# One sweep for the first layer's q, k and v, the norm chain moved ahead, and joined halves only from the memory's keys on

## The chip, the core and the metric

The kernel runs on one core of a Trainium2 chip. The metric is the device time of one execution in microseconds. TensorE (PE) multiplies, VectorE (DVE) and ScalarE (ACT) feed it and clear its results, POOL (GpSimd) does powers and some transfers, SP issues most loads.

## The reference

The program is a two-layer attention block followed by a hybrid mixer, a cross attention and an MLP, on 256 tokens of width 1024 in float32. The change touches the first layer, of which this is the core:

```python
h = rmsnorm(x, norm_gain[l])
mk, mv = jnp.split(memn @ w_mem_kv[l], 2, axis=-1)
...
qa, ka, va, qb, kb, vb, qm, gate = split_cols(h @ w_in_even[e], SPLIT_EVEN)
qa = rope_2d(rmsnorm(qa.reshape(B, S, A_HEADS, HEAD_DIM), q_norm_a[e]), grid_row, grid_col)
ka = rope_2d(rmsnorm(ka.reshape(B, S, A_KV, HEAD_DIM), k_norm_a[e]), grid_row, grid_col)
ya = global_gqa(qa, ka, va.reshape(B, S, A_KV, HEAD_DIM))
yb = window_gqa(...)
ym = memory_attn(qm.reshape(B, S, M_HEADS, M_HEAD_DIM), mk, mv)
y = jnp.concatenate([ya, yb, ym], axis=-1) * jax.nn.silu(gate)
x = x + y @ w_out_even[e]
```

## The kernel before

Each float32 operand is split in two: a high part rounded to the type that PE takes at full speed, and a low part, the difference. A product is then three matmuls: high x high, high x low, low x high (`mm3`). ACT writes the high part of a weight (`t_wh<-t_raw`), DVE the low part (`t_wl<-t_raw,t_wh`); both come from a weight tile `t_raw` that SP loads. There are three buffers for `t_raw` and four each for `t_wh` and `t_wl`; twenty-four slots of 4 KB hold the other operands.

Where the activations are the moving operand (`proj_t`), `merge` decides the form. With `merge` on, `proj_sum` lays the high and low part of the activations beside each other, so that one matmul of 512 columns does two of the three products and one of 256 columns the third; the two halves of the PSUM bank are then added by an ACT copy and a DVE add into `t_sum`. With `merge` off there are three matmuls of 256 columns into one place, and the readers take PSUM itself.

The first layer begins without the norm. The tokens come transposed (`t_xT`), two row blocks of 128 at a time, each followed by the weights of k, v and the window's v (384 columns, `t_mm` in two banks). `turn` multiplies by the norm's gain and splits (`t_gh<-t_xT,t_gT`). All eight row blocks are swept for these 384 columns, and later swept again for q (512 columns). The norm itself is applied to the results: squares of the tokens on ACT (`t_sq`), a sum and a reduce on DVE (`t_y<-t_sq`), a matmul with ones that sums over partitions (`t_at<-t_ones,t_y`), a power on POOL (`t_rstd`), and a matmul that spreads the result over partitions (`t_at<-t_p,t_ones`). From that DVE and ACT make the normed tokens `t_xs` and their halves `t_hT`, which the window's k (`kb`), the gate (`gate_tile`), and the memory's query (`mem_q`) use. `window_bias` makes a table with a one-hot matmul and stores it to DRAM. The rotations (`rope`) of k and q and the memory's norm are put between the projections in small steps.

The order of the instructions isn't the order in the text. `Plan` records all operations, then `order` puts them in a list with a cost model: each engine takes the ready operation of lowest priority number, which is the place in the text plus a `bias` and a `SHIFT` for a kind of tile. The list is issued as it stands, and each engine runs its part in order. Loads share one modelled queue with 450 ns each. Before the first data arrive, PE runs `WARM` matmuls on zeros.

Of the kernel before, what the change touches and what calls it, by code (L numbers as in the profile page):

```python
# [10 lines left out]
F32 = mybir.dt.float32  # L11
# [5 lines left out]
P = 128  # L17
# [12 lines left out]
class Plan:  # L30
# [13 lines left out]
    def __init__(self, nc):  # L44
        import concourse.bacc as bacc
        self.nc = nc
        self.names = bacc.Bacc("TRN2", target_bir_lowering=False, num_devices=1)
        self.ops, self.tiles, self.last, self.bias, self.ahead = [], {}, None, 0, False
        for e in self.ENGINES:
            setattr(self, e, Plan.Engine(self, e))  # L50
# [80 lines left out]
    def cost(self, engine, method, args, kwargs, outs, ins):  # L131
# [14 lines left out]
        if engine == "scalar":  # L146
            return n / 1.2 + (93 if sbuf else 51) + 94 * col + 93 * accum, 0.0, 0
# [14 lines left out]
    def order(self, prio):  # L162
# [12 lines left out]
        avail = {e: (2000.0 if e == "scalar" else 600.0, -1) for e in self.ENGINES}  # L175
        ring, bus = 0.0, 0.0
# [23 lines left out]
        while len(seq) < n:  # L200
# [19 lines left out]
            if o["bytes"]:  # L220
                if e != "gpsimd":
                    ring = max(ring, t) + 450.0
                    avail[e] = (ring, i)
                    bus = max(bus, ring + 650.0)
# [83 lines left out]
class Kernel:  # L308

    def __init__(self, ctx, tc, a, out):  # L310
        self.tc, self.nc, self.a, self.out = tc, Plan(tc.nc), a, out

        class Pool:

            def __init__(pool, name, bufs, space=None):
                pool.space = space
                pool.real = ctx.enter_context(tc.tile_pool(name=name, bufs=bufs, **({"space": space} if space else {})))

            def tile(pool, shape, dtype, tag=None, name=None, bufs=1):
# [12 lines left out]
        self.rate = 0.0  # L332
        self.merge = True
# [34 lines left out]
    def consts(self):  # L368
# [15 lines left out]
        early = self.work("st", [P, 8], 8)  # L384
        nc.scalar.activation(early, self.mhalf, AF.Exp)
        self.ident = self.c[:, C_ID:C_ID + P]

# [23 lines left out]
    def window_bias(self):  # L411
# [7 lines left out]
        oh = self.work("tanh", [33, 512], 2)  # L419
        nc.sync.dma_start(oh, a["onehot"])  # L420
        u = self.psum("at")
        uf = u.rearrange("p a b -> p (a b)")
        nc.tensor.matmul(uf[:8, :], rb, oh, start=True, stop=True)
        us = self.work("tanh", [8, 512], 2)
        nc.scalar.activation(us, uf[:8, :], AF.Copy, scale=-1.0)
        self.wb = self.dr.tile([8, 512], F32, name="wb")
        nc.sync.dma_start(self.wb, us)
# [108 lines left out]
    def spread(self, r, b):  # L536
# [274 lines left out]
    def gate_tile(self, w, c0, hT):  # L811
# [3 lines left out]
        for i in range(2):  # L815
            po = self.proj_t(w, c0 + i * 256, hT)
# [181 lines left out]
    def layer_even(self):  # L998
# [5 lines left out]
        def pieces():  # L1004
            for k0 in range(0, KT, 2):
                nc.ahead = True
                nc.sync.dma_start(self.xT[k0 // 4][:, k0 % 4:k0 % 4 + 2, :],
                                  a["x_t"][k0 * P:(k0 + 2) * P].rearrange("(k p) s -> p k s", p=P))
                nc.ahead = False
                raw = self.wp.tile([P, 2, 384], F32, tag="raw", name=self.name("raw"), bufs=3)  # L1010
                rs = slice(k0 * P, (k0 + 2) * P)
                for d, c0, n in ((0, 512, 256), (256, 1408, 128)):
                    nc.sync.dma_start(raw[:, :, d:d + n], w_in[rs, c0:c0 + n].rearrange("(k p) c -> p k c", p=P))
                turn(k0)
                turn(k0 + 1)
                yield k0, raw
                if k0 == TAB:
                    self.tab = self.rope_tables()

        po = self.proj_n(pieces(), KT, 384, xg)  # L1020
# [14 lines left out]
        self.window_bias()  # L1035
# [11 lines left out]
        pq = self.proj_n(self.wide(w_in, 0, KT, 0, step=2), KT, 512, xg)  # L1047
# [4 lines left out]
        kb = self.k_stack(self.proj_t(w_in, 1280, hT, P), 1)  # L1052
# [10 lines left out]
        g["a"] = self.gate_tile(w_in, 2048, hT)  # L1063
# [6 lines left out]
        self.flush("mem")  # L1070
        mk = self.mem_k(w_kv[0], self.mem1)
# [328 lines left out]
WARM = 20  # L1400
SHIFT = {("tensor", "mm"): 100, ("vector", "wl"): -20}
TAB = 4
BIAS = [40, 80, 110, 0, 0]
# [87 lines left out]
```

## Time and profile before

| | us |
|---|---|
| three runs | 779.42, 780.11, 781.4 (median 780.11) |
| the profiled execution | 779.68 |
| its span in the trace | 777.9 |
| PE busy | 763.1 (98%) |
| DVE busy | 620.0 (80%) |
| ACT busy | 536.8 (69%) |
| POOL busy | 74.7 (10%) |

The profiled execution's own time is 1.8 us above its span, for what lies around the instructions that the trace records. Nearly every operation is issued by one line of the program (L284), so rows are told apart by their tiles: `t_wl<-t_raw,t_wh` is the instruction that writes the low half of a weight. In a timeline row stand the start, the busy time, the engine, the operation, the shape, how many were merged into the row, and in brackets the idle time before it with what ended it. A matmul's busy time overlaps with the next, so its price is read from one start to the next.

### The profile page before, as it was taken

The numbers are of one execution on the slowest core, as the hardware profiler recorded it, in microseconds if no ns is written. First come the engines' busy times: TensorE is split into PE (matmuls) and PEld (weight loads), VectorE is DVE, ScalarE is ACT, GpSimd is POOL, SyncE is SP. The second block draws the span as 40 slices with busy tenths as digits, with TensorE's granted clock in tenths as the row PEclk, the third lists the DMA queues.
The fourth block names the chain that finished last, engine by engine and source line by source line (L and its number), as shares of the span: only waits on it lengthen the run. The fifth ranks groups of instructions, "written<-read, shape, count | busy, mean of one in ns | idle before, by whom it ended". The sixth has DMA issues, their size and how long they took to land.

```text
span 777.9 us, 11758 instructions
## 1 busy us (share of the span) xinstructions
PE 763.1 (98%) x4320; PEld 661.2 (85%) x4320; DVE 620.0 (80%) x1127; ACT 536.8 (69%) x1046; POOL 74.7 (10%) x105
## 2 busy tenths in 40 slices
PE   8989999999999999999999999999999999999996
PEld 7678898888888888888888898799989888888885
DVE  5999998998779889979988889976677655565554
ACT  6697987876679669757787787465556765556552
POOL 0640010000001421132011100100000000000000
PEclk9999999999999999999999999999999999999998
DMA  7796546445558855765348645356535565655631
GB/s 231 244 285 216 162 127 227 138 137 176 184 186 260 237 159 157 210 202 190 115 156 242 191 120 193 105 179 217 181 118 164 177 185 180 215 191 187 210 115 54
DMA packets 109989, 140.48 MB, mean 181 GB/s; under 512 B 3779, under 2 KB 81539, under 8 KB 109932
## 3 DMA queue, kind: packets, MB, share of 16 engines
q1 hardware_dynamic: 104460, 131.64, 52.5%
q0 software_dynamic: 5472, 8.10, 4.7%
q8 instruction: 34, 0.56, 0.3%
q14 instruction: 23, 0.19, 0.1%
HBM read 134.98 MB, written 1.06 MB: 175 GB/s over the span
## 4 chain that ended last, share of the span: by engine, by line
PE 86%; DVE 5%; issue 3%; POOL 2%; ACT 2%; DMA 1%; SPq 0%; POOLq 0%; DVEq 0%; ACTq 0%
PE t_mm L284 64%; PE t_at L284 22%; DVE t_wl L284 2%; DVE t_y L284 1%; POOL t_rrs L284 1%; POOL t_rstd L284 1%; DMA t_xT<-in_x_t_dram 1%; POOL t_ks L284 1%; ACT t_wh L284 0%; DVE t_xs L284 0%; DVE t_p L284 0%; DVE t_x L284 0%; ACT t_p L284 0%; ACT t_xg L284 0%; ACT t_mT L284 0%
## 5 line engine op out<-in xcount | busy, mean ns | idle before, releaser
L284 DVE TENSOR_TENSOR t_wl<-t_raw,t_wh 128x1024 fp32r<-128x1024 f32 (+1 forms) x237 | 288.8, 1219 | 72.6 <-ACT t_wh L284 70.9
L284 ACT ACTIVATE t_wh<-t_raw 128x1024 fp32r<-128x1024 f32 (+1 forms) x237 | 250.4, 1058 | 74.2 <-PE t_mm L284 61.3
L284 PE MATMUL t_mm<-t_mT,t_wh 128*128 128x512 f32 (+1 forms) x512 | 181.6, 394 | 0.4 <-ACT t_wh L284 0.4
L284 PE MATMUL t_mm<-t_mT,t_wl 128*128 128x256 f32 x496 | 131.9, 284 | 0.0
L284 PE MATMUL t_mm<-t_wh,t_yh 128*128 128x512 f32 x288 | 113.5, 394 | 0.0
L284 PE MATMUL t_mm<-t_wh,t_yl 128*128 128x512 f32 x288 | 112.9, 393 | 0.0
L284 PE MATMUL t_mm<-t_wl,t_yh 128*128 128x512 f32 x288 | 112.7, 391 | 0.0
L284 PEld LDWEIGHTS t_mm<-t_mT,t_wh 128*128 128x128 f32 x512 | 93.7, 188 | 14.0 <-ACT t_wh L284 0.8
L284 PEld LDWEIGHTS t_mm<-t_mT,t_wl 128*128 128x128 f32 x496 | 93.4, 189 | 6.5 <-DVE t_wl L284 0.3
L284 PE MATMUL t_at<-t_mT,t_wh 128*128 128x512 f32 (+1 forms) x256 | 85.7, 382 | 0.0
L284 ACT COPY t_sum<-t_mm 128x256 f32<-128x256 f32 x97 | 36.0, 371 | 55.6 <-PE t_mm L284 55.1
L284 PE MATMUL t_mm<-t_wh,t_gh 128*128 128x256 f32 (+2 forms) x256 | 65.9, 339 | 1.5 <-ACT t_wh L284 1.5
L284 PE MATMUL t_at<-t_mT,t_wl 128*128 128x256 f32 x240 | 63.8, 280 | 0.0
L284 PEld LDWEIGHTS t_mm<-t_wh,t_yl 128*128 128x128 f32 x288 | 54.1, 188 | 11.1
L284 PEld LDWEIGHTS t_mm<-t_wl,t_yh 128*128 128x128 f32 x288 | 54.1, 188 | 10.8
L284 PEld LDWEIGHTS t_mm<-t_wh,t_yh 128*128 128x128 f32 x288 | 54.1, 188 | 10.5 <-ACT t_yh L284 0.2
L284 PE MATMUL t_mm<-t_hT,t_wh 128*128 128x512 f32 x168 | 61.8, 400 | 1.0 <-DVE t_sum L284 1.0
L284 ACT ACTIVATE t_p<-t_p,t_st 128x256 f32<-128x256 f32 (+1 forms) x111 | 52.6, 493 | 9.6 <-DVE t_st L284 9.4
L284 POOL TENSOR_TENSOR t_rstd<-t_rstd,t_mhalf 128x2 f32<-128x2 f32 (+1 forms) x12 | 13.3, 1107 | 457.3 <-DVE t_rstd L284 457.3
L284 PEld LDWEIGHTS t_at<-t_mT,t_wh 128*128 128x128 f32 x256 | 45.8, 188 | 6.8
L284 DVE TENSOR_TENSOR t_sum<-t_mm,t_sum 128x256 f32<-128x256 f32 x97 | 40.8, 421 | 13.5 <-ACT t_sum L284 12.7
L284 PEld LDWEIGHTS t_mm<-t_wh,t_gh 128*128 128x128 f32 x256 | 45.1, 194 | 5.9 <-ACT t_wh L284 1.7
(177 smaller groups left out, 1389.1 us busy)
## 6 DMA issues: line engine op xcount, KB each, us to landing
t_raw<-in_w_in_odd_dram SPq DMA_DIRECT2D x20, 1024.0 KB, 5.2
t_raw<-in_w_up_dram SPq DMA_DIRECT2D x16, 1024.0 KB, 5.7
t_raw<-in_w_down_dram SPq DMA_DIRECT2D x16, 1024.0 KB, 5.0
t_raw<-in_w_in_dram SPq DMA_DIRECT2D x12, 1024.0 KB, 5.5
t_raw<-in_w_in_even_dram SPq DMA_DIRECT2D x10, 1024.0 KB, 5.1
t_raw<-in_w_mem_kv_dram SPq DMA_DIRECT2D x8, 1024.0 KB, 5.2
t_raw<-in_w_out_even_dram SPq DMA_DIRECT2D x6, 1024.0 KB, 5.6
t_raw<-in_w_out_odd_dram SPq DMA_DIRECT2D x6, 1024.0 KB, 5.3
```

The lines of the kernel that those rows point to most:

```text
L284: f(*[self.real(v) for v in args], **{k: self.real(v) for k, v in kwargs.items()})
```

## The change

The columns of both sweeps are taken in one pass: for each row block the 512 columns of q and the 384 of k and v, in four banks at once. The first two row blocks come one at a time, the first weight in two pieces; the gains and the first two blocks of tokens are loaded from ACT's queue, the rest of the tokens from SP's. The plan gives each engine its own load queue, starts ACT at 600 ns like the others, and charges the table load to the first activation. The norm chain has a bias of -200. `merge` starts off and is turned on before the first memory's keys. The projections of `kb` and of the gate write the banks named `at`. The one-hot matmul moves behind the gate. The diagonal of the spread may go to ACT or DVE. There are 24 warm-up matmuls instead of 20.

```diff
-        avail = {e: (2000.0 if e == "scalar" else 600.0, -1) for e in self.ENGINES}
-        ring, bus = 0.0, 0.0
+        avail = {e: (600.0, -1) for e in self.ENGINES}
+        ring, bus = {e: 0.0 for e in self.ENGINES}, 0.0
...
-        self.merge = True
+        self.merge = False
...
-        nc.sync.dma_start(self.g, a["gains"])
+        nc.scalar.dma_start(self.g, a["gains"])
         self.xT = [self.slot([P, 4, S], "xT", F32) for _ in range(2)]
+        for k in range(2):
+            self.load_x(k, 1, nc.scalar)
...
-            nc.vector.tensor_scalar(diag[:, t, :], self.ident, r[:, t:t + 1], None, ALU.mult)
+            self.scaled(diag[:, t, :], self.ident, r[:, t:t + 1])
...
-        po = self.proj_n(pieces(), KT, 384, xg)
+        def columns(k0, nk, c0=0, n=896):
+
+            raw = self.wp.tile([P, nk, n], F32, tag="raw", name=self.name("raw"), bufs=3)
...
+        pq, po = ([self.psum("mm", [P, 512]) for _ in range(2)] for _ in range(2))
+
+        def sweep(k, w, c0=0):
+
+            wh, wl = self.split(w)
+            for banks, b0, b1 in ((pq, 0, 512), (po, 512, 896)):
+                d0, d1 = max(b0 - c0, 0), min(b1 - c0, w.shape[1])
+                for t in range(2 if d0 < d1 else 0):
+                    ts = slice(t * P, (t + 1) * P)
+                    self.mm3(banks[t][:, :d1 - d0], xg(0, k)[:, ts], xg(1, k)[:, ts], wh[:, d0:d1], wl[:, d0:d1],
+                             k == 0, k == KT - 1)
+
+        for k0, nk in ((0, 1), (1, 1), (2, 2), (4, 2), (6, 2)):
...
+            if 0 < k0 < 6:
+                self.load_x(2 * ((k0 + 2) // 2), 2, nc.sync)
...
+        nc.bias = BIAS[5]
         sq = [self.slot([P, 4, S], "sq", F32) for _ in range(2)]
...
-        self.window_bias()
+        nc.bias = 0
+        spread_bias = self.window_bias()
...
-        pq = self.proj_n(self.wide(w_in, 0, KT, 0, step=2), KT, 512, xg)
...
-        kb = self.k_stack(self.proj_t(w_in, 1280, hT, P), 1)
+        kb = self.k_stack(self.proj_t(w_in, 1280, hT, P, tag="at"), 1)
...
-        g["a"] = self.gate_tile(w_in, 2048, hT)
+        g["a"] = self.gate_tile(w_in, 2048, hT, "at")
+        spread_bias()
...
         self.flush("mem")
+        self.merge = True
         mk = self.mem_k(w_kv[0], self.mem1)
...
-WARM = 20
+WARM = 24
-BIAS = [40, 80, 110, 0, 0]
+BIAS = [40, 80, 110, 0, 0, -200]
```

On ACT, near the start, the instructions before are these (`t_gh` the gained tokens, `t_sq` the squares):

```order
L284 ACTIVATE t_wh_123<-t_raw_88 128x768
L284 ACTIVATE t_gh_129<-t_xT_82,t_gT 128x256 x2
L284 ACTIVATE t_sq_138<-t_xT_82 128x1024
L284 ACTIVATE t_wh_148<-t_raw_100 128x768
L284 ACTIVATE t_gh_155<-t_xT_108,t_gT 128x256 x2
L284 ACTIVATE t_wh_164<-t_raw_114 128x768
```

And these now, from the second row block's weights (`t_wh_140`) to the third's (`t_wh_199`):

```order
L284 ACTIVATE t_wh_140<-t_raw_98 128x896
L284 ACTIVATE t_sq_150<-t_xT_84 128x1024
L284 ACTIVATE t_gh_159<-t_xT_84,t_gT 128x256 x2
L284 ACTIVATE t_sq_172<-t_xT_108 128x1024
L284 ACTIVATE t_gh_181<-t_xT_108,t_gT 128x256 x2
L284 ACTIVATE t_gh_189<-t_xT_108,t_gT 128x256 x2
L284 ACTIVATE t_wh_199<-t_raw_127 128x896
```

Both squares and the gained tokens of all blocks now stand between two weight splits that stood two instructions apart.

On DVE, the norm's sum and reduce stood behind all weight halves of the first sweep (`t_wl_197` is its last, `t_wl_233` the first of q):

```order
L284 TENSOR_TENSOR t_wl_197<-t_raw_141,t_wh_182 128x768
L284 TENSOR_TENSOR t_sq_138<-t_sq_138,t_sq_192 128x1024
L284 TENSOR_REDUCE t_y_221<-t_sq_138 128x256
L284 TENSOR_TENSOR t_wl_233<-t_raw_167,t_wh_210 128x1024
L284 TENSOR_SCALAR t_rstd_242<-t_at_237 128x2
```

Now they stand between the halves of the second and the third of eight row blocks (`t_wl_153` and `t_wl_209`):

```order
L284 TENSOR_TENSOR t_wl_153<-t_raw_98,t_wh_140 128x896
L284 SCALAR_TENSOR_TENSOR t_gh_159<-t_xT_84,t_gT,t_gh_159 128x256 x2
L284 TENSOR_TENSOR t_sq_150<-t_sq_150,t_sq_172 128x1024
L284 SCALAR_TENSOR_TENSOR t_gh_181<-t_xT_108,t_gT,t_gh_181 128x256
L284 TENSOR_REDUCE t_y_201<-t_sq_150 128x256
L284 TENSOR_TENSOR t_wl_209<-t_raw_127,t_wh_199 128x896
L284 TENSOR_SCALAR t_rstd_219<-t_at_212 128x2
```

The reduce moved ahead of six weight halves. On PE the token sums (`t_at_212`) moved with it, into the third row block:

```order
L284 MATMUL t_mm_146<-t_wh_199,t_gh_159 128x512
L284 MATMUL t_mm_155<-t_wh_199,t_gh_159 128x512
L284 MATMUL t_at_212<-t_ones,t_y_201 128x1 x2
L284 MATMUL t_mm_161<-t_wh_199,t_gh_159 128x384
L284 MATMUL t_mm_168<-t_wh_199,t_gh_159 128x384
L284 MATMUL t_mm_146<-t_wl_209,t_gh_159 128x512
```

Before, they stood in q's sweep, behind its first matmul:

```order
L284 MATMUL t_mm_136<-t_wl_197,t_gh_172 128x384
L284 MATMUL t_mm_136<-t_wh_182,t_gh_172 128x384
L284 MATMUL t_mm_235<-t_wh_210,t_gh_110 128x512
L284 MATMUL t_at_237<-t_ones,t_y_221 128x1 x2
L284 MATMUL t_mm_240<-t_wh_210,t_gh_110 128x512
```

So the token sums have come forward from behind the whole first sweep to the third of eight row blocks, and what follows them on PE is queued behind the reduce.

On SP, the weights of the gate and of the memory's query, and the memory's rows between them, stand as follows now (`t_raw_371` and `t_raw_451` are the query's two halves):

```order
L284 DMA t_raw_305<-in_w_in_even_dram 128x8x256
L284 DMA t_raw_371<-in_w_in_even_dram 128x8x256
L284 DMA t_memraw_401<-in_mem_dram 128x2x512
L284 DMA t_memraw_408<-in_mem_dram 128x2x512
L284 DMA t_memT_413<-in_mem_t_dram 128x4x256
L284 DMA t_memT_425<-in_mem_t_dram 128x4x256
L284 DMA t_cst<-in_const_dram 128x320
L284 DMA t_x<-in_x_dram 128x2x1024
L284 DMA t_raw_451<-in_w_in_even_dram 128x8x256
```

Before, the same row of transfers, with the store of the bias table ahead of it:

```order
L284 DMA t_wb<-t_tanh_337 8x512
L284 DMA t_raw_377<-in_w_in_even_dram 128x8x256
L284 DMA t_raw_401<-in_w_in_even_dram 128x8x256
L284 DMA t_memraw_441<-in_mem_dram 128x2x512
L284 DMA t_memraw_449<-in_mem_dram 128x2x512
L284 DMA t_memT_458<-in_mem_t_dram 128x4x256
L284 DMA t_memT_467<-in_mem_t_dram 128x4x256
L284 DMA t_cst<-in_const_dram 128x320
L284 DMA t_x<-in_x_dram 128x2x1024
L284 DMA t_raw_491<-in_w_in_even_dram 128x8x256
```

The store is gone from this place, it now follows the first memory's key weights; the rest is in the same order.

More of the change, by code (lines that the diff above doesn't have):

```diff
@@ L47, in __init__ @@
         self.names = bacc.Bacc("TRN2", target_bir_lowering=False, num_devices=1)
-        self.ops, self.tiles, self.last, self.bias, self.ahead = [], {}, None, 0, False
+        self.ops, self.tiles, self.last, self.bias, self.ahead, self.table = [], {}, None, 0, False, 0.0
         for e in self.ENGINES:
@@ new lines, in sweep @@
+        def sweep(k, w, c0=0):
[7 more added lines that the diff above has]
+        for k0, nk in ((0, 1), (1, 1), (2, 2), (4, 2), (6, 2)):
+            if k0 == 0:
+                parts = [(c0, columns(0, 1, c0, n)) for c0, n in ((0, 512), (512, 384))]
+            else:
+                parts = [(0, columns(k0, nk))]
+            if 0 < k0 < 6:
+                self.load_x(2 * ((k0 + 2) // 2), 2, nc.sync)
+            for j in range(nk):
+                turn(k0 + j)
+                for c0, raw in parts:
+                    sweep(k0 + j, raw[:, j, :], c0)
+            if k0 == TAB:
+                self.tab = self.rope_tables()
```

59 lines of the change are left out of this document (29 added, 30 removed).

## The prediction

> **What bounds the kernel now.** I read the page first, then the busy time in stretches of 5 us, then TensorE's timeline of the first 70 us, then the groups of instructions that feed it.
>
> ```profile
> span 777.9 us, 11758 instructions
> PE 763.1 (98%) x4320; PEld 661.2 (85%) x4320; DVE 620.0 (80%) x1127; ACT 536.8 (69%) x1046; POOL 74.7 (10%) x105
> PE 86%; DVE 5%; issue 3%; POOL 2%; ACT 2%; DMA 1%; SPq 0%; POOLq 0%; DVEq 0%; ACTq 0%
> ```
>
> TensorE (PE) is busy 98% and carries 86% of the chain that ended last. So the change can only gain where PE waits, and PE waits mostly in the first 60 us. In the stretches below the columns are busy us (and instructions) of PE, weight loads, VectorE (DVE), ScalarE (ACT) and POOL, then the granted clock, the DMA share and GB/s.
>
> ```profile
> 0.00:5.00 5.00, 3.71 (x17) 3.71 (x18) 0.27 (x1) 2.30 (x4) 0.80 (x8) 1.00 0.55 145
> 5.00:10.00 5.00, 3.14 (x14) 2.61 (x13) 2.46 (x5) 3.14 (x6) 0.00 (x0) 0.88 0.99 312
> 10.00:15.00 5.00, 5.00 (x25) 5.00 (x24) 4.58 (x8) 4.41 (x8) 0.00 (x0) 0.78 0.67 188
> 25.00:30.00 5.00, 4.31 (x17) 2.61 (x16) 4.99 (x11) 4.80 (x8) 1.31 (x3) 1.00 0.69 217
> 35.00:40.00 5.00, 4.27 (x25) 3.33 (x23) 4.91 (x9) 4.13 (x9) 2.78 (x3) 1.00 1.07 367
> 45.00:50.00 5.00, 5.00 (x32) 4.41 (x32) 4.96 (x12) 4.70 (x11) 1.45 (x3) 1.00 1.13 322
> ```
>
> Up to 10 us the loads are late (DVE only 2.46 busy); then the clock is down for some 3.4 us; from 25 us on DVE is full (4.99, 4.91, 4.96 of 5) and PE waits for it.
>
> ```profile
> 1.29 4.46 PE L284 MATMUL t_at<-t_warm 128*128 128x256 f32 x20 [1.29 <-POOL t_warm L284]
> 7.24 0.62 PE L284 MATMUL t_mm<-t_wh,t_gh 128*128 128x384 f32 x2 [1.49 <-ACT t_wh L284]
> 8.23 0.44 PE L284 MATMUL t_mm<-t_wl,t_gh 128*128 128x384 f32 x1 [0.37 <-DVE t_wl L284]
> 8.89 0.53 PE L284 MATMUL t_mm<-t_wl,t_gh 128*128 128x384 f32 x1
> 9.21 0.53 PE L284 MATMUL t_mm<-t_wh,t_gh 128*128 128x384 f32 x1
> 12.69 0.33 PE L284 MATMUL t_mm<-t_wh,t_gh 128*128 128x384 f32 x1
> 12.87 0.33 PE L284 MATMUL t_mm<-t_wl,t_gh 128*128 128x384 f32 x1
> 26.26 1.01 PE L284 MATMUL t_at<-t_tanh,t_rb 33*8 33x512 f32 x2 [0.69 <-POOL t_sink L284]
> 32.02 0.62 PE L284 MATMUL t_mm<-t_wh,t_gh 128*128 128x512 f32 x2
> 32.47 0.39 PE L284 MATMUL t_mm<-t_wl,t_gh 128*128 128x512 f32 x1
> 32.93 0.39 PE L284 MATMUL t_mm<-t_hT,t_wh 128*128 128x512 f32 x1
> 40.29 0.47 PE L284 MATMUL t_mm<-t_hT,t_wh 128*128 128x512 f32 x1 [1.02 <-DVE t_sum L284]
> 44.75 0.38 PE L284 MATMUL t_mm<-t_hT,t_wl 128*128 128x256 f32 x1 [0.99 <-DVE t_wl L284]
> 48.46 0.39 PE L284 MATMUL t_mm<-t_hT,t_wh 128*128 128x512 f32 x1
> 48.69 0.28 PE L284 MATMUL t_mm<-t_hT,t_wl 128*128 128x256 f32 x1
> 48.80 0.39 PE L284 MATMUL t_mm<-t_hT,t_wh 128*128 128x512 f32 x1
> 66.49 0.40 PE L284 MATMUL t_mm<-t_gh,t_wh 128*128 128x512 f32 x1
> ```
>
> Matmuls overlap, so I take the time from one start to the next: 0.18 us for 384 columns at full clock (12.69 to 12.87) against 0.32 in the dip (8.89 to 9.21), 0.23 for 512 (two in 32.02 to 32.47), 0.23 and 0.11 to 0.12 for the two of a joined pair (48.46, 48.69, 48.80). Both sweeps run from 7.24 to 32.93, that is 25.7 us; 48 x 0.175 + 48 x 0.23 = 19.4 us would do. The next stretch, the projections on hT, is 32.93 to 66.49, 33.6 us. It holds 72 joined pairs x 0.35 = 25.2 us, 16 score matmuls of 256 columns and a dozen of 128, which I estimate at 2.8 us, so it loses 5.6 us.
>
> The feeding instructions, by form, in the first 70 us:
>
> ```profile
> L284 DVE TENSOR_TENSOR t_wl<-t_raw,t_wh 128x1024 fp32r<-128x1024 f32 x15 | 18.2, 1216 | 0.1
> L284 DVE TENSOR_TENSOR t_wl<-t_raw,t_wh 128x768 fp32r<-128x768 f32 x4 | 3.8, 955 | 2.8 <-ACT t_wh L284 2.8
> L284 DVE TENSOR_TENSOR t_sum<-t_mm,t_sum 128x256 f32<-128x256 f32 x9 | 3.8, 418 | 0.1
> L284 DVE SCALAR_TENSOR_TENSOR t_gh<-t_xT,t_gT,t_gh 128x256 fp32r<-128x256 f32 x8 | 3.5, 482 | 4.9 <-ACT t_gh L284 4.9
> L284 DVE TENSOR_REDUCE t_y<-t_sq 128x256 f32<-128x1024 f32 x1 | 2.0, 2015 | 0.0
> L284 DVE TENSOR_TENSOR t_sq<-t_sq,t_sq 128x1024 f32<-128x1024 f32 x1 | 1.2, 1219 | 0.0
> ```
>
> ```profile
> L284 ACT ACTIVATE t_wh<-t_raw 128x1024 fp32r<-128x1024 f32 x17 | 18.1, 1062 | 4.0 <-DMA t_raw<-in_w_in_even_dram 1.8 <-PE t_mm L284 1.8 <-DMA t_raw<-in_w_mem_kv_dram 0.3
> L284 ACT ACTIVATE t_gh<-t_xT,t_gT 128x256 fp32r<-128x256 f32 x8 | 3.6, 497 | 2.6 <-DMA t_xT<-in_x_t_dram 2.6
> L284 ACT ACTIVATE t_wh<-t_raw 128x768 fp32r<-128x768 f32 x4 | 3.3, 832 | 1.2 <-DMA t_raw<-in_w_in_even_dram 1.2
> L284 ACT ACTIVATE t_sq<-t_xT 128x1024 f32<-128x1024 f32 x2 | 2.1, 1042 | 0.0
> L284 ACT ACT_TABLE_LOAD x1 | 1.3, 1283 | 0.7 <-PEq L1476 0.7
> ```
>
> A split of 896 columns lies between the rows of 768 and 1024: 0.95 us on ACT, 1.09 on DVE.
>
> **Term 1, the sweep: 0.8 us gained.** The warm-up row gives 0.21 us a matmul; 24 of them end at 1.29 + 24 x 0.213 = 6.4 us, and the first projection follows at once if its operands are there. First operands: 0.43 MB; before moved 145 x 5 = 0.73 MB by 5 us, so they lie there by about 4.3. ACT issues three transfers and loads its table (1.28) by about 3.5, hidden under that landing; behind the landing come a split of 512 (0.6) and two t_gh (1.0). That ends before 6.4, with about 0.5 us to spare.
>
> Row block k=0 runs 6.4 to 8.8 (6 x 0.23 + 6 x 0.175 = 2.43 us). Block k=1 needs 1.22 MB, at 5 + 0.49/0.312 = 6.6 us, plus 0.95 on ACT: ready at 7.6, before 8.8. It ends at 11.2. Then it stalls. After that second split ACT has, in its order, two squares (2.1), six t_gh (3.0), and only then the split for k=2: 7.6 + 5.1 + 0.95 = 13.6 us. Its data (2.93 MB, with all of x ahead of it, at 10 + 0.64/0.312 = 12.1) are there sooner; the squares are not hidden here. On DVE the sum of squares ends at 11.9, t_gh at 12.4, the reduce (2.0) at 14.4, and the low half of k=2 at 15.5. PE does two matmuls at 13.6, waits at the token sums for the reduce, does two more, and waits for 15.5: idle 3.3 of the 4.3 us from 11.2. Each later block has its halves 1 us or more ahead of PE, since DVE delivers one in 1.1 us and PE takes 2.4. Bounds of the stall: 1.9 (if the reduce were not in the way) to 4.2.
>
> The clock: before, 1.49 + 0.37 us of idle ahead of the dip brought 3.4 us at about half clock, 1.7 us lost. The new stall is longer, so I expect a second dip; it may begin while PE still waits, hence 1.2 us, bounds 0 and 1.7. [...]
>
> The constants and the identity now travel behind the whole sweep's weights, and the spread of the norm needs the identity; with the hT operands that PE then needs from DVE I allow 0.5 us (0 to 2). Sum: 6.4 + 19.4 + 3.3 + 1.2 + 0.5 + 0.4 (token sums, spread) = 31.2 us, against 32.93 less the one-hot matmul's 0.9 (26.26 to about 27.2), which now comes later and costs the same there: 32.0. Gain 0.8, bounds -1.9 and 3.9.
>
> The load through two queues gains little more than this: before, the first loads sat behind each other's issue, but PE's warm-up ends at 6.4 whatever they do.
>
> **Term 2, the projections on hT: 1.8 us gained.** 72 joined pairs become 216 matmuls of 256 columns. At 0.12 for 256 columns three of them take 0.36 against 0.35 of the pair: 72 x 0.01 = 0.7 us lost (at 0.11 it would be as much gained, and that is the other bound). Nine copies on ACT and nine adds on DVE (3.8 us, row above) go, and the reads of their results become reads of PSUM of the same size. PE's wait of 1.02 us for a bank that an add frees goes; so does the 0.99 for a weight half, as hT and the halves are made during the sweep. Of the 5.6 us lost I take 2.5 back: these two, and 0.5 of the small pauses. 2.5 - 0.7 = 1.8. Bounds: nothing back, if the q rotation (now after the gate, on a full DVE) stands in front of the weight halves instead, and all 5.6.
>
> Further edits with one answer: the spread of the diagonal may go to ACT (one of two does); the bias table's matmul, copy and store move past five weight loads and the memory's rows on SP, and nothing reads the table before the window heads, which come after the memory's; the store waits on SP for ACT's copy with a weight behind it that waits for its own slot anyway. The rest, from the first memory's keys to the end, keeps joined pairs and, after the first layer, the same order on all engines, on a PE that is 98% busy; it starts earlier and keeps the gain.
>
> **Sum.** 0.8 + 1.8 = 2.6 us. The profiled execution took 779.68 us with a span of 777.9; its 779.68 - 2.6 = 777.1. The median of the three runs is 780.11, 0.43 above that execution, so 777.5. A difference of 0.3% (2.3 us) is about what a measurement of this kernel can tell.
>
> **Rivals.**
>
> ```profile
> DMA to landing us min/median/max: 3.3/5.0/14.7
> DMA to landing us min/median/max: 8.6/8.6/8.6
> ```
>
> [...] Chance 0.2.
>
> (b) DVE is no longer last anywhere before the memory's keys, all 5.6 us come back: 777.5 - 3.1 = 774.4. For it: 3.8 us less on DVE. Against it: DVE was full from 25 us on, and what it does for the rotations stays. Chance 0.12.
>
> (c) Slower. The second weight load of the memory query stands on SP behind both memories' rows, constants and x. Before, that weight took 14.7 us to land and the transposed memory 8.6 (the two rows above, of t_raw and t_memT in the first 60 us). Now the whole train waits for the slot that the kb weights' split frees, about 29 us by my reckoning. PE reaches that query half at about 31.2 + 7 x 8 x 0.36 + 0.7 = 52, its weight lands at about 33 + 14.7 = 47.7 and needs 2.3 us of splitting: 2 us of slack. DVE, in order, also waits for the transposed memory ahead of the k rotation. If hT is late and that split comes at 36.5 instead of 29, PE loses 7.5 - 2 = 5.5 us: 783.0. It decides from about 31 us on. Chance 0.14.
>
> (d) The saving is handed back: the q rotation and query stacks, now after the gate, fill DVE between 50 and 70 us as before. Term 2 is -0.7, term 1 stays: 780.0. Chance 0.14.
>
> **Chances and range.** The forecast keeps 0.40. Faster by over 0.3% (under 777.8): two thirds of the forecast, nearly all of (a), all of (b): 0.55. Slower by over 0.3% (above 782.4): most of (c) and a little of (d): 0.16. Within: 0.29. The range for 8 in 10 runs from 774.0, below (b), to 781.8, beyond (d), leaving out most of (c).
>
> **What would show it.** The first projection at about 6.4 us; k=2's first matmul at 13 to 14 with ACT's t_wh as releaser; a granted clock under 0.9 in 10 to 20; the last of the sweep at 31 to 32; no PE wait for t_sum before the memory's keys; those keys begin before 60 us. Wrong, if DVE's or ACT's idle time grows at t_memT or t_raw between 40 and 55 us, or if the sweep ends after 33.

## The result and the profile after

The changed kernel took 779.43 us in the median of 12 executions (777.27 to 782.85), the kernel before 780.08 beside it (779.21 to 783.25). The ratio is 0.9995, 95% interval 0.9981 to 1.0008: no difference that this measurement can tell. The forecast of 777.5 is 1.9 us too low; the measured time lies inside its range.

The page of the profiled execution (779.23 us), in the same lines as before the change:

```profile
span 777.5 us, 11899 instructions
PE 763.6 (98%) x4396; PEld 665.2 (86%) x4396; DVE 618.4 (80%) x1114; ACT 535.1 (69%) x1043; POOL 76.2 (10%) x105
PE 88%; DVE 6%; ACT 2%; issue 2%; DMA 1%; POOL 1%; SPq 0%; POOLq 0%; ACTq 0%
```

Busy time in stretches of 5 us (PE, weight loads, DVE, ACT, POOL, then granted clock, DMA share, GB/s):

```profile
5.00:10.00 5.00, 5.00 (x25) 3.99 (x24) 3.32 (x7) 3.68 (x7) 0.00 (x0) 1.00 0.98 325
10.00:15.00 5.00, 2.46 (x11) 1.57 (x9) 3.77 (x5) 4.34 (x7) 0.00 (x0) 1.00 1.03 384
15.00:20.00 5.00, 4.91 (x18) 4.13 (x19) 4.80 (x8) 2.31 (x3) 3.74 (x3) 0.66 0.68 212
35.00:40.00 5.00, 5.00 (x42) 5.00 (x42) 4.49 (x10) 4.35 (x11) 3.00 (x6) 1.00 1.07 368
45.00:50.00 5.00, 5.00 (x37) 4.01 (x36) 4.35 (x15) 4.52 (x13) 3.11 (x5) 1.00 1.10 342
```

TensorE's hole has moved from 5 to 10 us (3.14 busy before) to 10 to 15 (2.46), with the low clock behind it again; from 35 to 50 us TensorE is now full (4.27 before in 35 to 40). TensorE's timeline at the hole, where the memory's keys begin, and at the one long pause further on:

```profile
14.00 0.73 PE L284 MATMUL t_mm<-t_wh,t_gh 128*128 128x512 f32 x2 [2.27 <-ACT t_wh L284]
15.09 0.60 PE L284 MATMUL t_at<-t_ones,t_y 128*128 128x1 f32 x4 [0.36 <-DVE t_y L284]
60.10 0.40 PE L284 MATMUL t_mm<-t_gh,t_wh 128*128 128x512 f32 x1
293.07 0.36 PE L284 MATMUL t_at<-t_ph,t_vp 128*128 128x256 f32 x1 [1.15 <-DVE t_st L284]
```

Where the time went: for each matmul I take the time to the next start, less the spacing of its shape at full clock, as in the prediction, and add up by stretch. This is an estimate: other roundings of the spacings move a row by about half a microsecond, and the last row by several, alike in both kernels.

| us of the span | TensorE time lost before | after |
|---|---|---|
| 0 to 10 | 3.1 | 0.3 |
| 10 to 20 | 1.4 | 4.9 |
| 20 to 62 | 8.0 | 1.9 |
| 62 to 80 | 0.6 | 3.0 |
| 260 to 300 | 0.9 | 2.4 |
| all others | 22.3 | 21.9 |

That is 36.3 before and 34.4 after, 1.9 less; the change also gives TensorE 1.4 us more to do (4 warm-ups, 0.85; 72 pairs taken apart, 0.58). 0.5 us are left, which is what the two profiled executions differ by (779.68 and 779.23). So the change does its work in the first 62 us: 5.4 us less lost, 4.0 when the added work is taken off, with the new hole at 10 to 20 already in it. Behind that it hands most of it back: 2.4 us between 62 and 80, and 1.5 at one pause near 291.

### The profile page after: what moved, and what is told of

The parts are those of the page before. It is cut to its first block, busy times and chain, and to the rows that moved or that the text cites. A ratio compares the mean times of both kernels' runs of the same rounds, so it can differ in the third digit from the quotient of the medians.

```text
span 777.5 us, 11899 instructions
## 1 busy us (share of the span) xinstructions
PE 763.6 (98%) x4396; PEld 665.2 (86%) x4396; DVE 618.4 (80%) x1114; ACT 535.1 (69%) x1043; POOL 76.2 (10%) x105
## 4 chain that ended last, share of the span: by engine, by line
PE 88%; DVE 6%; ACT 2%; issue 2%; DMA 1%; POOL 1%; SPq 0%; POOLq 0%; ACTq 0%
PE t_mm L284 64%; PE t_at L284 24%; DVE t_p L284 1%; DVE t_wl L284 1%; DVE t_y L284 1%; ACT t_wh L284 1%; DMA t_xT<-in_x_t_dram 1%; POOL t_rrs L284 1%; DVE t_x L284 1%; DMA t_gT<-in_gains_dram 0%; DVE t_qs L284 0%; ACT t_p L284 0%; DVE t_xg L284 0%; POOL t_rstd L284 0%; ACT t_xg L284 0%
## 5 line engine op out<-in xcount | busy, mean ns | idle before, releaser
L284 DVE TENSOR_TENSOR t_wl<-t_raw,t_wh 128x1024 fp32r<-128x1024 f32 (+2 forms) x238 | 289.3, 1218 | 75.8 <-ACT t_wh L284 74.0
L284 ACT ACTIVATE t_wh<-t_raw 128x1024 fp32r<-128x1024 f32 (+2 forms) x238 | 249.7, 1053 | 78.1 <-PE t_mm L284 63.8
L284 ACT COPY t_sum<-t_mm 128x256 f32<-128x256 f32 x88 | 32.6, 371 | 48.7 <-PE t_mm L284 48.2
L284 PE MATMUL t_mm<-t_hT,t_wh 128*128 128x512 f32 (+1 forms) x160 | 48.4, 357 | 0.0
L284 PEld LDWEIGHTS t_at<-t_mT,t_wl 128*128 128x128 f32 x240 | 45.3, 189 | 3.2
```

The source lines that it names most:

```text
L284: f(*[self.real(v) for v in args], **{k: self.real(v) for k, v in kwargs.items()})
```

## The experiments

All times are medians; each kernel ran in alternation with the kernel before on its chip, whose medians were 780.53, 780.52 and 780.63 in the three groups. Differences between kernels of different groups are taken from the ratios (0.001 is 0.78 us); the changed kernel's is 0.9995.

| kernel | us | ratio to before, 95% interval |
|---|---|---|
| chain late | 780.84 | 1.0003, 0.9995 to 1.0012 |
| joined all | 783.00 | 1.0033, 1.0021 to 1.0045 |
| stall filled | 786.27 | 1.0080, 1.0066 to 1.0093 |
| table moved | 779.90 | 0.9993, 0.9980 to 1.0006 |
| loads by need | 778.17 | 0.9968, 0.9957 to 0.9980 |
| three fixes | 777.32 | 0.9954, 0.9938 to 0.9971 |
| split only | 777.05 | 0.9955, 0.9939 to 0.9971 |
| stall filled 2 | 776.58 | 0.9953, 0.9937 to 0.9969 |
| joined filled | 781.80 | 1.0009, 0.9996 to 1.0021 |
| before, longer warm-up | 779.40 | 0.9989, 0.9977 to 1.0001 |
| filled, two fixes | 777.44 | 0.9963, 0.9947 to 0.9979 |
| split, two fixes | 779.18 | 0.9981, 0.9970 to 0.9992 |

**1. The norm chain.**

```diff
-BIAS = [40, 80, 110, 0, 0, -200]
+BIAS = [40, 80, 110, 0, 0, 0]
```

> The changed kernel with the norm chain's bias put back from -200 to 0: the squares and the token sums are planned in their old rank, everything else stays. Theory A (the chain in front of the third row block is what stalls TensorE there): the first projection of k=2 comes at about 11.5 instead of 14.0 us, the pause of 2.3 us goes, and the sweep ends some 3 us earlier; time about 777. Theory B (the third block's weights land late, at 12.5 us, whatever the chain does, because the rest of x travels ahead of them): the pause stays within 0.5 us of 2.3; only VectorE's reduce (2.0 us) leaves the place between the two halves, so the low half of k=2 comes about 1 us earlier, and hT comes some 4 us later, which the interleaved projections pay; time 779 to 781.

780.84. This kernel's timeline, TensorE's first matmul of the third row block and then ScalarE ahead of it:

```profile
14.69 1.33 PE L284 MATMUL t_mm<-t_wh,t_gh 128*128 128x512 f32 x4 [3.02 <-ACT t_wh L284]
...
11.00 0.91 ACT L284 ACTIVATE t_gh<-t_xT,t_gT 128x256 fp32r<-128x256 f32 x2 [1.06 <-DMA t_xT<-in_x_t_dram]
11.81 1.99 ACT L284 ACTIVATE t_sq<-t_xT 128x1024 f32<-128x1024 f32 x2
13.70 0.93 ACT L284 ACTIVATE t_wh<-t_raw 128x896 fp32r<-128x896 f32 x1
```

The pause is there all the same (3.02 us, first projection of k=2 at 14.69). But the bias doesn't move the squares: the planner puts them in front of the split either way (11.81, the split at 13.70), so this run leaves theory A's cause in place and can't refute it. The changed kernel's own trace says more. Its ScalarE, in the same stretch, and the load that its split for k=2 needs:

```profile
10.45 1.06 ACT L284 ACTIVATE t_sq<-t_xT 128x1024 f32<-128x1024 f32 x1 [0.66 <-DMA t_xT<-in_x_t_dram]
11.41 1.69 ACT L284 ACTIVATE t_gh<-t_xT,t_gT 128x256 fp32r<-128x256 f32 x4
13.01 1.78 ACT L284 ACTIVATE t_wh<-t_raw 128x896 fp32r<-128x896 f32 x2
...
L284 SPq DMA_DIRECT2D t_raw<-in_w_in_even_dram x1: 397/397/397, 5.6 to 5.6; - x1
DMA to landing us min/median/max: 6.9/6.9/6.9
```

The load was issued at 5.6 and landed 6.9 us later, at 12.5; the split began at 13.01. So the work in front of it on ScalarE held it up by 0.5 of the 2.27 us, and the late load by the rest: theory B in the main. What the chain's earlier place is worth by itself (779.43 against 780.84) is not settled, as the two intervals overlap.

**2. The form of hi and lo, on the new sweep.**

```diff
-        self.merge = False
+        self.merge = True
```

> The changed kernel with hi and lo joined in every projection, those ahead of the first memory's keys too, as before the change. Theory A (the separate form is worth term 2 of the prediction): nine ScalarE copies and nine VectorE adds (3.8 us) come back ahead of the keys, TensorE waits for t_sum and for weight halves again, time about 1.8 us longer, 781. Theory B (VectorE's adds there are hidden once the projections lie inside the sweep, and the separate form costs TensorE 0.6 us of work): time 0 to 0.6 us shorter, 778.8.

783.00: 0.0038 above the changed kernel, 3.0 us, well over what theory A gave. The adds are not hidden.

**3. The form alone, on the old sweep.**

```diff
-        self.merge = True
+        self.merge = False
...
         self.flush("mem")
+        self.merge = True
         mk = self.mem_k(w_kv[0], self.mem1)
```

> The kernel before with one part of the change alone: hi and lo separate until the first memory's keys, joined from there on; sweep, loads and chain as before the change. Theory A (the separate form carries most of the change's gain): VectorE loses nine adds and ScalarE nine copies between 33 and 66 us, 2.5 to 3.5 us come back there, time about 777.5 on a kernel before of 780.2. Theory B (it needs the sweep in one piece, since in the old order the projections wait for weights and not for adds): at most 1 us, 779.2 to 780.2.

777.05, 3.5 us faster than before: theory A. What TensorE waited for between 33 and 64 us (us in total, times, longest), first before, then with the separate form:

```profile
PE t_mm L284 <- DVE t_wl L284: 1.2, 2, 1.0
PE t_mm L284 <- DVE t_sum L284: 1.0, 1, 1.0
```

```profile
PE t_at L284 <- DVE t_p L284: 0.5, 1, 0.5
PE t_mm L284 <- DVE t_wl L284: 0.4, 1, 0.4
```

So this one small part of the change does more than the whole of it. With experiments 2 and 3 all four corners are there: the form is worth 3.5 us on the old sweep (1 to 0.9955) and 3.0 on the new (1.0033 to 0.9995); the sweep with its loads and chain costs 2.6 us with joined pairs (1 to 1.0033) and 3.1 without (0.9955 to 0.9995). Within the intervals, about 1 us each, the two parts add up.

In the two profiles this gain is not a matter of the low clock. The execution with the separate form had it too, though the views show 1.00 (the third number from the end) in both of these stretches:

```profile
7.23:10.64 3.41, 3.41 (x10) 2.92 (x11) 2.68 (x5) 3.41 (x7) 0.00 (x0) 1.00 1.07 350
10.64:14.06 3.42, 3.42 (x21) 3.42 (x20) 3.42 (x7) 3.12 (x5) 0.00 (x0) 1.00 0.69 193
```

TensorE is full in both, with 10 matmuls of 384 columns in the first and 21 in the second: about 0.34 us each up to 10.64, as in the dip of the kernel before (0.32), and 0.16 behind it. The trace's records of the clock begin only at 10.64, and the views count what lies ahead of the first record as full: in the kernel before they show 1.00 up to its first record at 5.41 us, where its warm-up matmuls are 0.21 us apart. By the reckoning of lost time above, this profile loses 3.0 us less than the kernel before between 20 and 62 us, and only 0.4 less ahead of that.

**4. What the sweep costs: the low clock.** First try, dummy work in the hole that the planner counts as work:

```diff
...
+            if k0 == 1:
+                busy = self.psum("at")
+                nc.bias = 300
...
+                for _ in range(NFILL):
+                    nc.tensor.matmul(busy[:, 0, :], self.warm[:, :P], self.kept[:, :S], start=True, stop=True)
+                nc.bias = 0
...
+NFILL = 20
```

> The changed kernel with 20 matmuls of the zero tile against the second block's low weight half (256 columns, results not read, 2.1 us at full clock) between the second and the third row block, where TensorE stood idle for 2.3 us. Theory A (the idle time brings the half clock that follows it): the granted clock stays at 1.00 from 10 to 20 us, the third block still starts at about 14, and all after it comes 1.5 to 1.7 us earlier; about 777.7. Theory B (the half clock follows from something else, the age of the program or the load, not from idle time): it comes all the same, for 3.4 us, and the time stays at 779.4 or gets longer.

786.27, and it answers nothing: the planner put the norm chain later behind that work, TensorE waited 2.82 us for t_p and 2.84 for hT between 32 and 38 us, and a low clock of 6.8 us followed. At 12.85 to 16.26 TensorE was 2.16 of 3.41 us busy, and the low clock came at 16.26.

Second try: 28 of them, planned at no cost, so that all else keeps the order of the changed kernel.

```diff
...
+                for i in self.idle_work:
+                    o = nc.ops[i]
+                    o["cost"], o["forms"] = 0.0, [(*o["forms"][0][:4], 0.0)]
```

> The changed kernel with 28 matmuls of the zero tile against the second block's low weight half (256 columns, results not read, 3.0 us at full clock) in the pause ahead of k=2, all other instructions of all engines in the same order. In the traces so far the half clock came for the next 3.41 us whenever TensorE was busy for 39% or less of a stretch of 3.41 us, and not at 51% or more; these stretches begin at another time after the start in each execution. Theory A (that share is what decides): no stretch falls under 0.6, no half clock before the end of the program, and the kernel runs like the changed kernel's executions without it, 777.3 to 778.0, all in a narrow spread. Theory B (the half clock comes from something that the dummy matmuls don't change): it stays at 14 to 20 us, 779 to 782 as before.

776.58, the fastest kernel of this study: work whose result nobody reads, put where TensorE had nothing to do, takes 0.0042 off, 3.3 us.

```profile
11.38 3.48 PE L284 MATMUL t_at<-t_wl,t_warm 128*128 128x256 f32 x28
15.33 0.73 PE L284 MATMUL t_mm<-t_wh,t_gh 128*128 128x512 f32 x2 [0.46 <-ACT t_wh L284]
```

K=2 starts no sooner for it (15.33 us in its profile, 14.00 in the changed kernel's); what differs there is the clock. Not all of the 3.3 is shown to be the clock's: its profile lacks the pause near 291 too, and the changed kernel's own executions with the highest mean clock (below) took 777.3 to 778.7, not 776.6. Here are whole stretches of 3.41 us of the clock, in the kernel before, the changed one, "joined all" and this one (columns as above; the clock is the third number from the end):

```profile
5.41:8.82 3.41, 1.55 (x8) 1.02 (x8) 1.64 (x4) 1.86 (x4) 0.00 (x0) 1.00 1.02 323
8.82:12.23 3.41, 3.41 (x13) 3.41 (x12) 2.22 (x6) 3.41 (x6) 0.00 (x0) 0.50 0.69 225
```

```profile
9.07:12.48 3.41, 2.66 (x12) 1.95 (x11) 1.93 (x4) 2.75 (x6) 0.00 (x0) 1.00 1.03 375
12.48:15.89 3.41, 1.53 (x8) 1.04 (x8) 3.41 (x4) 2.77 (x5) 0.00 (x0) 1.00 1.05 389
15.89:19.30 3.41, 3.41 (x11) 2.82 (x10) 3.41 (x6) 1.33 (x2) 3.04 (x1) 0.50 0.48 144
```

```profile
9.22:12.64 3.42, 2.08 (x11) 1.57 (x9) 2.96 (x5) 2.85 (x6) 0.00 (x0) 1.00 1.03 386
12.64:16.05 3.41, 1.25 (x8) 1.16 (x9) 2.52 (x4) 1.79 (x2) 0.00 (x0) 1.00 1.05 373
16.05:19.46 3.41, 3.41 (x11) 3.04 (x10) 3.29 (x5) 1.79 (x2) 1.63 (x2) 0.50 0.45 131
```

```profile
11.09:14.50 3.41, 3.41 (x30) 3.41 (x29) 1.63 (x3) 2.72 (x6) 0.00 (x0) 1.00 1.04 382
14.50:17.91 3.41, 2.58 (x14) 1.65 (x13) 3.41 (x4) 2.99 (x4) 0.31 (x1) 1.00 0.70 248
```

The traces record the clock in stretches of 3.41 us: one at full and one at half clock in the kernel before (from 5.41 and 8.82 us), three at full (10.24 us) and one at half in the changed one (from 5.65 and 15.89). In the first 48 to 55 us of all fourteen profiles a stretch recorded at full clock with 1.55 us or less of TensorE's busy time is followed by one at half clock, and one with 2.08 (above, "joined all") or more is not, except for the 2.16 of the try above; so busy time alone doesn't fix it. (The 39% and 51% of the expectation count a matmul by its columns at full-clock spacing, in the first 50 us, and can't be set beside these.) The stretches begin at another time in each execution (one begins at 5.41 us before, 5.65 in the changed kernel, 4.26 in this one), so the same hole sometimes falls into one stretch and sometimes is cut in two (0.66 us busy in one in "chain late", 2.08 and 1.25 in two in "joined all"). That shows in the changed kernel's 12 executions, by the mean clock of each: 777.3, 777.6 and 778.7 us at 0.997 to 0.999; 778.5 to 779.7 at 0.995 and 0.996; 779.6 to 782.9 at 0.993 and 0.994. In seven of the eight executions with dummy work it was 0.997 or 0.998, 776.2 to 777.6; in the eighth 0.996, 780.5. One stretch at half clock takes 0.0022 off this mean, so I read the three groups as none, one and two stretches. It is a rough measure: the last 4.5 us of the profile before and the last 3.8 of the changed kernel's, where TensorE is done (at 770.8 and 770.4), are at half clock too, and a half clock ahead of the first record isn't counted (experiment 3).

**5. The sweep without the low clock.** Experiment 2 with the 28 dummy matmuls.

> Sweep, loads and norm chain of the change, hi and lo joined everywhere as before it (the second experiment, 783.0), and 28 dummy matmuls in the pause ahead of k=2, every other instruction in the same order. It shows what the sweep is worth by itself once the half clock is out of it, to be set against the kernel before (780.5). Theory A (the sweep loses only through the half clock that its pause brings, one or two stretches of 1.7 us each): no half clock, 780 to 780.8, so the sweep alone is worth nothing or a little. Theory B (it loses elsewhere, in the projections that now share VectorE with hT and the rotations): 781.5 to 783.

781.80, no low clock in its profile: 0.0024 or 1.9 us better than without the dummies, but not under before (0.7 us above, interval -0.3 to 1.6). The time lies in theory B's range, by the ratio (781.2 on 780.5) between the two: the low clock was 1.9 of the sweep's 2.6 us here, but without it the sweep is still not faster than before. Its waits of TensorE between 50 and 80 us, and below them VectorE's load there (third busy number):

```profile
PE t_mm L284 <- DVE t_wl L284: 2.0, 3, 1.0
PE t_mm L284 <- DVE t_gh L284: 1.0, 1, 1.0
PE t_at L284 <- ACT t_p L284: 0.5, 1, 0.5
PE t_mm L284 <- ACT t_p L284: 0.3, 1, 0.3
```

```profile
50.00:60.00 10.00, 9.26 (x53) 7.46 (x52) 9.94 (x24) 7.38 (x13) 3.62 (x7) 1.00 0.74 216
60.00:70.00 10.00, 7.71 (x45) 6.08 (x46) 9.83 (x19) 4.96 (x8) 0.71 (x1) 1.00 0.23 79
```

VectorE is full to 9.8 or 9.9 of 10 us: q's rotation, which the new order puts behind the gate, takes 6.1 us there between 50 and 80 (0.7 in the kernel before) and meets the memory's halves and the adds. In the changed kernel three of the seven adds of these 30 us are gone and the same two stretches show 9.12 and 9.79; it loses 3.0 us at 62 to 80, this one 4.8. Before, the two stretches show 8.78 and 10.00 and only 0.6 us are lost, so a full VectorE goes with the loss but doesn't prove it.

**6. The hole's cause.** Loads in the order of need:

```diff
-        for k0, nk in ((0, 1), (1, 1), (2, 2), (4, 2), (6, 2)):
+        for k0, nk in ((0, 1), (1, 1), (2, 1), (3, 1), (4, 2), (6, 2)):
...
-            if 0 < k0 < 6:
-                self.load_x(2 * ((k0 + 2) // 2), 2, nc.sync)
+            if k0 in XAT:                   # {1: 2, 3: 4, 4: 6}
+                self.load_x(XAT[k0], 2, nc.sync)
...
+            if nk == 1:
+                raw = self.slot([P, 1, n], "raw", F32)
...
```

> The changed kernel with the sweep's loads in the order in which TensorE needs them: row blocks 0 to 3 as four loads of one block each, in buffers of their own, x's columns 4 and 5 behind block 3 and columns 6 and 7 behind blocks 4 and 5, instead of all of x ahead of a load of blocks 2 and 3 together. The norm chain keeps its bias of -200 and follows the loads of x. Theory A (the pause ahead of k=2 is the late landing of that load, and the half clock follows from the pause): the first projection of k=2 comes by 11.5 us instead of 14.0, no half clock between 8 and 21 us, about 4 us of the 4.9 lost between 10 and 20 come back; time 775 to 776.5, and in a narrow spread, since no run can catch a half clock. Theory B (ScalarE's squares and VectorE's reduce, wherever they now stand, are next and make the same pause a block later): a pause of 1.5 us or more between 12 and 20 us; time 778 to 779.5.

778.17 in a narrow spread (777.17 to 779.01, mean clock 0.997 or 0.998 in all nine executions). TensorE's timeline and stretches:

```profile
11.24 0.57 PE L284 MATMUL t_mm<-t_wh,t_gh 128*128 128x384 f32 x2
11.66 0.39 PE L284 MATMUL t_mm<-t_wl,t_gh 128*128 128x512 f32 x1
20.60 0.61 PE L284 MATMUL t_at<-t_ones,t_y 128*128 128x1 f32 x4 [1.09 <-DVE t_y L284]
24.15 0.71 PE L284 MATMUL t_at<-t_p,t_ones 128*128 128x128 f32 x4 [0.60 <-ACT t_p L284]
```

```profile
10.00:15.00 5.00, 5.00 (x26) 4.47 (x25) 3.28 (x5) 3.04 (x6) 0.00 (x0) 1.00 1.05 375
20.00:25.00 5.00, 3.80 (x21) 3.19 (x22) 3.92 (x8) 1.12 (x3) 5.00 (x11) 1.00 0.84 268
```

The hole and its low clock are gone: k=2 follows k=1 without a pause, at 11.4 us. So the order of the loads made the hole, as the trace in experiment 1 has it. (With the loads, ScalarE's order moved too: one square and one `t_gh` now stand ahead of this split, which starts at 9.32. So this run alone doesn't part the two.) But the later columns of x make the norm chain later, and TensorE now waits for its sums, its spread and hT (1.5, 1.3 and 2.0 us lost in the stretches 10 to 20, 20 to 30 and 30 to 40, where the changed kernel lost 4.9, 0.4 and 0.1). Each theory has half.

**7. The pause near 291 us.** Two transfers moved on POOL's queue, nothing else (the order in words, not code):

```diff
-  POOL: load 1, 4 additions, load 2, 4 additions
+  POOL: load 1, load 2, 4 additions, 4 additions
```

> The changed kernel, every engine in the same order but for two transfers on POOL's queue: the second group of the second layer's position table is loaded ahead of the first group's additions instead of behind them. Theory A (at 280 to 286 us POOL's four additions of the table, 8 us late since their load landed late, run beside VectorE's six scalings of t_p and slow them from 0.35 to about 0.9 us, and TensorE's pause of 1.3 us at 291.5 follows from that): the scalings are back at 0.35 to 0.45 us, the pause goes, and the time is 1 to 1.3 us shorter, 778.2. Theory B (VectorE's chain is late there for another reason): the additions move, but the pause stays and so does the time, 779.4.

VectorE's scalings of t_p between 278 and 287 us (min, median, max in ns), after the change and in this kernel; under the first, POOL's additions in the changed kernel:

```profile
L284 DVE TENSOR_SCALAR t_p<-t_p,t_st x8: 335/656/1040, 278.3 to 285.1; 128x256 f32<-128x256 f32 x8
...
282.03 3.93 POOL L284 TENSOR_TENSOR t_rpbe<-t_cst,t_rpbraw 128x384 f32<-128x384 f32 x4 [7.19 <-DVE t_p L284]
```

```profile
L284 DVE TENSOR_SCALAR t_p<-t_p,t_st x8: 329/345/349, 279.7 to 284.9; 128x256 f32<-128x256 f32 x8
...
278.84 2.00 POOL L284 TENSOR_TENSOR t_rpbe<-t_cst,t_rpbraw 128x384 f32<-128x384 f32 x2 [3.69 <-DVE t_st L284]
```

The mechanism holds: the four scalings that start during one of POOL's additions (3.93 / 4 = 0.98 us) take 0.96 to 1.04 us instead of 0.34, and with the additions out of the way the pause is gone. The time is not: 779.90. In this kernel's profile another pause has come, 1.03 us at 514.96 for ScalarE's t_xn, which neither the profile of the changed kernel nor that of before shows: ScalarE's weight split ahead of that t_xn waited 2.05 us here and 0.70, for its load, in the changed kernel. And in "stall filled 2", whose POOL keeps the changed kernel's order, the pause near 291 is missing as well. The kernel before has that order on POOL too; its second group of the table landed by 278.2 us, the changed kernel's by 281.8. So single pauses of about 1 us come and go between nearly the same programs. In the changed kernel's trace the four slow scalings start 0.11 to 0.18 us behind the start of an addition and end 0.15 to 0.16 us behind its end; before, two that start within an addition's last half microsecond end 0.15 us behind it and take 0.45 and 0.63 us.

**8. Before, with a longer warm-up** (27 instead of 20, planned at no cost).

> The kernel before with 27 instead of 20 warm-up matmuls, so that TensorE is fed from 5.7 us up to its first projection at 7.2, every other instruction in the same order. Theory A (its half clock at 8.8 to 12.2 follows from that pause, but is hidden, since the loads and VectorE's halves that follow would make TensorE wait anyway): no half clock in any execution, and the time within 0.5 us of 780.5. Theory B (it costs what it costs after the change, 1.7 us a stretch): about 1 us faster in the median, 779.5 or less.

779.40 is theory B's figure, but the ratio (0.9 us faster, interval 1.8 faster to 0.1 slower) leaves room for no gain: not settled. The low clock did not come at 8.8 us, but in the profile another hole, 2.33 us ahead of the matmul that waits for the one-hot table's load, brought one at 28.3 (the stretch ahead of it had 1.42 us of work). The change has moved that matmul to 46.50, where no such pause is seen; the prediction counted the move as costing the same.

**9. More of the same** (the table's load moved, and pairs joined only from the first memory's gate on), on three kernels:

> The loads by need of the run before, the position table's second load moved ahead of the first additions, and hi and lo joined only from the first memory's gate on, instead of from its keys on, so that eight ScalarE copies and eight VectorE adds more go while VectorE is full (60 to 80 us). Theory A: 62 to 80 us loses some 1.5 us less than the 2.9 of the changed kernel, no pause near 291; time about 1 to 2 us under that of the loads alone. Theory B (what VectorE no longer adds there it does for the scores; other pauses of 1 us come at random in one execution and not in the next): the same time as the loads alone within 0.5 us.

> The changed kernel with the 28 dummy matmuls (776.58), the position table's second load ahead of the first additions, and hi and lo joined from the first memory's gate on. Theory A: the two fixes are worth about 0.9 us, as between the loads by need with and without them (778.17 and 777.32): 775.7. Theory B (that difference was chance of single pauses): 776.4 to 776.8.

> The kernel before with hi and lo separate until the first memory's gate, and the position table's second load ahead of the first additions; sweep, loads and chain as before the change. Theory A: 0.9 us below the separate form alone (777.05): 776.2, by two edits and without any of the sweep. Theory B: 776.8 to 777.3.

0.9954 after 0.9968, 0.9963 after 0.9953, 0.9981 after 0.9955. The first by itself looks like theory A, the other two go the other way: no gain that holds. In the stretch from 62 to 80 us, where 1.5 us less were expected to be lost, the profiles lose 2.3 against 2.6 us (loads by need) and 2.1 against 2.9 (filled). The last kernel had a mean clock of 0.992 to 0.996 in 10 of 12 executions; in its profile the pause ahead of the first projection was 2.82 us (1.27 in the separate form alone) and two stretches at half clock followed, to 14.43. So part of what sets those two apart may be the low clock falling differently; how much stays open, since the mean clock leaves out what lies ahead of its first record (experiment 3).

## Why the prediction was right or wrong

- **First projection at 6.4, k=2 at 13 to 14 with t_wh as releaser, a low clock behind it:** right (6.18; 14.00; 0.50 from 15.89 to 19.30). The size of the stall was right as well: 4.9 us lost at 10 to 20, less 1.7 for the clock, is 3.2, against 3.3. But the reason given, ScalarE's squares in front of the split, was the smaller part, 0.5 us: the load landed at 12.5, 6.9 us after its issue, and with the loads in order of need the hole goes. That 13 to 14 us came out is luck.
- **Term 1, 0.8 us gained:** wrong in sign, and outside its bounds (-1.9): the sweep with its loads and chain costs 2.6 to 3.1 us on either form of the pairs. Two steps failed. The low clock was put at one dip of 1.2 us that costs the same in each execution; it comes for none, one or two stretches, and the dummy work that takes it out gains 1.9 us with joined pairs (3.3 with separate ones, not all of it the clock's). The larger step, by the joined pairs, is one put at nothing: what the new order costs behind the sweep. Without the dip the term gives 2.0 us gained (0.8 and the 1.2); with the dummy work the joined kernel stands 0.7 above the kernel before, so 2.7 us are missing. They fit the stretch from 62 to 80, where the joined kernel loses 4.8 us and the kernel before 0.6, with q's rotation now on VectorE: the term ended at the sweep. That VectorE is the cause stays an argument; taking more adds off it (experiment 9) brought no gain that holds.
- **Term 2, 1.8 us gained:** right in sign and mechanism, too small: 3.0 to 3.5. Of the 5.6 us that the prediction saw lost there it took back 2.5. With the form alone, TensorE's waits for t_sum and the 1.0 us wait for t_wl went as named, and of the small pauses more than the 0.5 allowed: the stretch 30 to 62 loses 3.1 us instead of 6.0.
- **The sum:** 2.6 forecast, 0.65 measured (780.08 - 779.43; 0.4 by the ratio). One term was 3.4 to 3.9 too high and one 1.2 to 1.7 too low: the range held by luck, by two errors that partly cancel.
- **Rivals.** (a) no dip: true of some executions, by their mean clock, which I put down to where the stretches of 3.41 us happen to begin; those took 777.3 to 778.7, not 776.3, and in the profile the pause of 2.27 us was followed by the low clock. (b) all waits ahead of the keys gone: true from 20 to 62 us, 8.0 us lost before and 1.9 after, but paid for on both sides of it. (c) the query's second half: issued at 35.1, landed 14.5 us later at 49.7, as priced, and TensorE lost only 1.5 us in all from 40 to 62; the slack held. (d) handed back by q's rotation on a full VectorE: true in part, 2.4 us between 62 and 80; its 780.0 is the nearest to the measured time, but term 2 itself did not turn to a loss.
- **"Keeps the same order and the gain" to the end:** false. The gain was 1.7 us at the second layer's norm (199.45 before, 197.74 after) and 0.5 at the end: two loads that took 7.6 us to land, against 3.4 and 5.0 before, brought POOL's additions onto VectorE's scalings.
- **Markers.** The keys at 60.10 were just late of "before 60". The idle time at t_memT or t_raw did not come. "The sweep ends after 33" would have said wrong for no reason: its last matmul started at 35.70, because hT's projections are woven into it from 26.70 on.

## What to carry to other kernels

Ask of every pause how much of one clock stretch (3.41 us here) it leaves empty: a pause of 1.5 us (before) and one of 2.3 (after) on TensorE cost their own length and one stretch at half clock in the profiles, two stretches in that of "table moved", and dummy matmuls in it gained 1.9 and 3.3 us in two kernels. When a change has separable parts, cost and try each alone: here one small part gained 3.5 us and the rest gave 3.1 back. And where a change moves work on the feeding engines to a later stage, as q's rotation here, the sum must go on to that stage. Do not read a clock of 1.00 at the start of a profile without the spacing of the matmuls beside it.

## What was not expected of the hardware

- Half clock after a stretch of 3.41 us in which TensorE was still busy for up to 1.55 us (the kernel before), once for 2.16 ("stall filled"); it came in steps of one or two whole stretches (3.41 or 6.83 us).
- At the start the matmuls ran at half speed too: 0.21 us from one warm-up matmul of 256 columns to the next, against 0.12 from 5.71 us on in the changed kernel. In all fourteen profiles the 3.41 us ahead of the first record of the clock hold 10 to 18 matmuls, where a full stretch of 256 columns behind it holds 30 ("stall filled 2"). That first record comes between 4.2 and 10.64 us, and the views show 1.00 up to it all the same.
- Matmuls of a zero tile count as work for it: with 28 of them the stretch from 11.09 to 14.50 us is full (3.41 us) and the clock stays at 1.00 behind it ("stall filled 2").
- VectorE's scaling of 128x256 in SBUF takes 0.34 us alone ("table moved") and up to 1.04 beside POOL's addition of 128x384 (the changed kernel).
- The time of a load from issue to landing differs by 2.6 to 4.2 us between two executions of nearly the same program: the two loads of the position table's second group took 3.4 and 5.0 us before and 7.6 each after.
